# A decoder trunk: last pass of an output projection and its LayerNorms moved into the recurrent stage, with three PSUM banks for its last pieces

## Chip, cores and metric

The kernel runs on one core of a Trainium2 chip. The metric is device time in microseconds. Positions in the trace ("at 1926") are microseconds from the start of the profiled execution's span.

## What is computed

A trunk of two layers over 1024 tokens of width 1024, in float32. Layer 0 mixes tokens by attention, layer 1 by an RWKV-7 recurrence with 12 heads beside 4 memory heads. Each layer merges its heads by an output projection, and each sublayer ends in a LayerNorm:

```python
o = jnp.concatenate([y, o_mem], axis=-1)      # 768 + 256 columns
mix = o @ w_out[1]                            # (1024, 1024)
x = layer_norm(ALPHA * x + mix, ln1_g[1], ln1_b[1])
ff = jnp.square(jax.nn.relu(x @ w_ff1[1])) @ w_ff2[1]
x = layer_norm(ALPHA * x + ff, ln2_g[1], ln2_b[1])
```

Every float32 operand of a matmul is split into a high and a low part, and a product is three matmuls (high by high, high by low, low by high).

## The kernel before

A planner orders the instructions of each engine at build time by program order and its own estimate of when they are ready; each engine's queue is then run in order. `issue_after(m)` queues what it encloses behind `m` on that engine. SyncE (SP) issues the DMAs.

**The recurrent stage** (`rwkv`, L656 to L1246) runs 12 units n = 0 to 11 (two head pairs by 256 tokens). Unit n is prepared two steps ahead (`prepare`, `early`, `late`, `bonus`), its blocks are merged one step ahead (`merge`, PSUM pool `psi`, two banks), then `sequence(n)` runs the recurrence and `finish(n)` (L1188) writes normalised outputs to `o_d` in DRAM. All eight PSUM banks are taken: `psm` 1, `psg` 2, `psi` 2, `psq` 2, `psx` 1.

**Pieces.** Independent work for TensorE is drawn from the generator `project()`: 40 input projections, 16 memory-attention steps and the 48 pieces of `first_out` (L730). `fill(n)` draws n pieces; the table `FILL` (L34) says how many in each unit: 12 before the stage, `FILL[12]` = 7 before the loop, then `FILL[n]` = 4, 4, 3, 4, 4, 4, 11, 11, 12, 12, 11, 6, and `fill(99)` for the rest. All use the one bank of `psm`.

**The output projection.** `first_out` makes three passes over the residual rows `R` (two tiles of 128 x 4 x 1024), with two of the eight 128-row blocks of `w_out` each: blocks 0, 1, then 2, 3, then 6, 7 ("third group"). For each of eight row tiles tt and two column halves nh, `out_part` (L1248) makes one piece: six matmuls of 512 columns (`mm3`, L149 to L151), then one add into `R` (L1255 or L1257). Blocks 4, 5 belong to the last units; their weights are loaded and split after all pieces (L1243), and the rows of `o_d` fetched (`fetch_o`, L345 to L349: a DMA into a `raw` buffer, then `split`: a cast on ScalarE, L143, and a subtraction on VectorE, L144). `raw` buffers: two (`wr`); split pairs for weights: two (`wp`).

**The last pass** runs in the next stage, `out_and_ff` (L1276), layer 1: `out_row` (L1260) does both halves into a double bank of the pool `pso` (two of them) with one add of 1024 columns (L1271). After each second row tile `norm` (L1383) runs `normalise2` on a pair of row tiles: four statistics (L217), two aggregates (L218), 14 small operations (L220 to L228) on VectorE, two scalings on ScalarE (L230), and a store to `n_d`. For the first four row tiles `first_half` adds transposes (`columns`, L241, with copies on ScalarE, L244) and splits. `ahead` loads and splits the first weights of the feed-forward into the memory of `R`'s first half, and `second_half` transposes the rest, with early products pinned between.

The lines that decide the order before:

```python
                fill(99)
                self.wo = [self.load_split(...) for k in (4, 5)]
                for kt in (4, 5):
                    self.fetch_o(kt, kt - 2, slice(0, QT * 3))
```

Of the kernel before, what the change touches and what calls it, by code (L numbers as in the profile page):

```python
# [10 lines left out]
F32 = mybir.dt.float32  # L11
# [9 lines left out]
P = 128  # L21
T = 1024
# [44 lines left out]
class Trunk:  # L67
# [588 lines left out]
    def rwkv(self, rows_src):  # L656
# [8 lines left out]
        with ExitStack() as so:  # L665
# [43 lines left out]
            def project():  # L709
# [15 lines left out]
                yield from remember()  # L725
                yield from first_out()


            def first_out():
                R = self.R = Halves(self.x_tile("h", 1, F32), self.x_tile("l", 1, F32))  # L730
                self.Xh, self.Xl = Halves(self.x_tile("h", 0)), Halves(self.x_tile("l", 0))
                for ks, src in (((0, 1), 0), ((2, 3), 2), ((0, 1), 6)):
                    for k in ks:
                        self.fetch_o(src + k % 2, k)
                    wo = [self.load_split(a["w_out"][1, (src + k % 2) * P : (src + k % 2 + 1) * P, :], (1024,)) for k in ks]
                    for tt in range(KT):
                        if src == 0:
                            nc.sync.dma_start(R[:, tt, :], res_src[tt * P : (tt + 1) * P, :])
                        for nh in range(2):
                            self.out_part(psm, R, tt, nh, ks, wo, src == 0)  # L740
                            yield 1


# [56 lines left out]
            def fill(n):  # L800
                for _ in range(n):
                    if next(pieces, 0) == 0:
                        break
# [99 lines left out]
                psms[:] = [psm]  # L903
            with ExitStack() as s:
                kp = pool(s, "k")
                lp = pool(s, "ld", 2)
                tp = pool(s, "t")
                up = pool(s, "u", 2)
                psg = pool(s, "psg", 2, space=PSUM)
                psi = pool(s, "psi", 2, space=PSUM)  # L910
                psq = pool(s, "psq", 1, space=PSUM)
# [13 lines left out]

                cmp_ = kp.tile([P, P], F32, name="cmpk")
                self.pad(kp, 96)
                self.pad(tp, 96)
                ARK = [kp.tile([P, 2, NC, 2, P], F32, name=f"ARK{i}") for i in range(2)]
                nc.gpsimd.memset(cmp_, 0.0)  # L930
# [256 lines left out]
                def finish(n):  # L1187
                    d = DU.pop(n)  # L1188
                    pa, gs = d["pa"], d["gs"]
                    y8 = d["yd"].rearrange("p u c i -> p (u c) i")  # L1190
                    gt = tp.tile([P, 2, QT], F32, name="gt")
                    nc.sync.dma_start(gt, lo_d[pa : pa + 2].rearrange("u (j i) t -> i u j t", i=P)[:, :, 2, gs])
                    mn = sm.tile([P, 8], F32, name="mn")
                    vr = sm.tile([P, 8], F32, name="vr")
                    nc.vector.tensor_reduce(mn, y8, axis=AX.X, op=ALU.add)
                    nc.vector.tensor_scalar(mn, mn, 1.0 / CH, None, op0=ALU.mult)
                    nc.vector.tensor_sub(y8, y8, mn[:, :, None].broadcast_to([P, 8, CH]))
                    ysq = tp.tile([P, 8, CH], F32, name="ysq", tag="o")
                    nc.scalar.activation(ysq, y8, AF.Square)
                    nc.vector.tensor_reduce(vr, ysq, axis=AX.X, op=ALU.add)  # L1200
                    nc.vector.tensor_scalar(vr, vr, 1.0 / CH, 64e-5, op0=ALU.mult, op1=ALU.add)
                    rs2 = self.rsqrt(vr, 8, "gn")
                    nc.vector.tensor_mul(y8, y8, rs2[:, :, None].broadcast_to([P, 8, CH]))
                    o = tp.tile([P, 2, QT], F32, name="o", tag="o")
                    po = psg.tile([P, 2, NC, CH], F32, name="ps_yo", tag="g")
                    for u in range(2):
                        for c in range(NC):
                            for R, hd in HD:
                                nc.tensor.matmul(po[R, u, c, :], d["yd"][R, u, c, :], self.ident[R, R], start=True, stop=True)
                    for u in range(2):  # L1210
                        j = pa + u
                        nc.scalar.activation(c3(o[:, u, :]), po[:, u], AF.Identity, scale=self.col("gng", j), bias=self.col("gnb", j))
                    nc.vector.tensor_add(o, o, d["bv"])
                    nc.vector.tensor_mul(o, o, gt)
                    nc.sync.dma_start(self.o_d[pa * P : (pa + 2) * P, gs].rearrange("(u i) t -> i u t", i=P), o)
# [12 lines left out]
                for n in range(N):  # L1228
                    sequence(n)
                    if n + 1 < N:  # L1230
                        merge(n + 1, steps[1])
                    if n + 2 < N:
                        prepare(n + 2)
                        early(n + 2)
                        late(n + 2)
                    finish(n)
                    if n + 2 < N:
                        bonus(n + 2)
                    for c, m in enumerate(anchors):
                        with self.tc.issue_after(m):  # L1240
                            fill((FILL[n] + c) // NC)
                fill(99)
                self.wo = [self.load_split(a["w_out"][1, k * P : (k + 1) * P, :], (1024,)) for k in (4, 5)]  # L1243
                for kt in (4, 5):
                    self.fetch_o(kt, kt - 2, slice(0, QT * 3))


    def out_part(self, psm, R, tt, nh, ks, wo, first):  # L1248
        nc = self.nc
        ts_, ns = slice(tt * P, (tt + 1) * P), slice(nh * H, (nh + 1) * H)  # L1250
        ps = psm.tile([P, H], F32, name="ps_o", tag="mm")
        for k, (wh, wl) in zip(ks, wo):
            self.mm3(ps, self.Xh[:, k, ts_], self.Xl[:, k, ts_], wh[:, ns], wl[:, ns], k == ks[0], k == ks[-1])
        if first:
            nc.vector.scalar_tensor_tensor(R[:, tt, ns], R[:, tt, ns], ALPHA, ps, op0=ALU.mult, op1=ALU.add)  # L1255
        else:
            nc.vector.tensor_add(R[:, tt, ns], R[:, tt, ns], ps)  # L1257
# [17 lines left out]

    def out_and_ff(self, layer, res_src, res_dst, last, R=None):  # L1276
        nc, a = self.nc, self.a
        n_d = self.dp.tile([T, D], F32, name=f"n_d{layer}")
# [8 lines left out]
        with ExitStack() as s:  # L1287
# [10 lines left out]
            with ExitStack() as s1:  # L1298
# [70 lines left out]
                with ExitStack() as s2:  # L1369
# [11 lines left out]


                    def norm(tt):  # L1383
                        chain.append(self.normalise2(rows_of(tt)))
                        nc.sync.dma_start(n_d[tt * P : (tt + 2) * P, :].rearrange("(t p) d -> p t d", p=P), rows_of(tt))

                    def first_half(tt):
                        cs, es, i = span(tt)
                        norm(tt)
# [27 lines left out]
                    if R is None:  # L1417
# [9 lines left out]
                        for h in (0, 4):  # L1427
                            for tt in range(h, h + 4):
                                self.out_row(pso, R, tt, range(4), wo, True)
                            for tt in range(h, h + 4):  # L1430
                                self.out_row(pso, R, tt, range(4, 8), wo[4:], False)
                                if tt % 2:
                                    (first_half if tt < 4 else norm)(tt - 1)
                            if h == 0:
                                ahead(0)
                                ahead(1)
                    else:
                        K1 = new(0), new(1)
                        region = lambda i: self.x_tile("hl"[i], 1)

                        self.fetch_o(4, 2, slice(QT * 3, T))
                        self.fetch_o(5, 3, slice(QT * 3, T))
                        for tt in range(KT):
                            self.out_row(pso, R, tt, (2, 3), self.wo, False)
                            if tt % 2:
                                (first_half if tt < 4 else norm)(tt - 1)
                            if tt == 3:
                                ahead(0)
                                ahead(1)
                    s4.close()  # L1450
                    psB = pool_of(s1)("psB", 4, space=PSUM)
                    cut = lambda t, c: (t[0][:, :, c], t[1][:, :, c])
# [477 lines left out]
```

## Time and profile before

| | |
|---|---|
| median of 3 runs | 2670.86 us (2668.06 to 2672.97) |
| profiled execution | 2670.26 us, span 2667.5 us |
| busy share of the span | TensorE 94%, weight loads 76%, VectorE 68%, ScalarE 45%, GpSimd 8% |
| recurrent stage, until its last piece | about 1380 to 1966 us |
| last pass and first LayerNorms | 1966 to 2021 us |

An engine's busy time counts its instructions; matmuls overlap, so a busy TensorE is not one at its peak. In a timeline row stand the start, the time of the (merged) instructions, the engine, the line, the operation, output and inputs, shapes and count, and in brackets the idle time of the engine before it with what ended it.

### The profile page before, as it was taken

What the parts mean: (1) busy time and instruction counts of PE and PEld (TensorE: products, weight loads), DVE (VectorE), ACT (ScalarE), POOL (GpSimd) and SP (SyncE); (2) the same over time, 40 slices, a digit from 0 to 9 for tenths busy, and PEclk for the clock granted to TensorE, in tenths of its full rate; (3) what the DMA queues carried; (4) which work ended last, traced back from release to release, by engine and by line L of the source; (5) the groups of instructions that cost most, each with busy time, mean ns of one, the idle gap of its engine ahead of it and who ended that gap; (6) DMA issues with size and microseconds to landing.
All of it is one profiled execution on the core that took longest, in us unless ns stands there. A gap on an engine that the chain in (4) does not pass through costs nothing. (4 is left out here: it accounts for less than half of the span.)

```text
span 2667.5 us, 41854 instructions
## 1 busy us (share of the span) xinstructions
PE 2519.3 (94%) x16189; PEld 2034.7 (76%) x16189; DVE 1804.9 (68%) x3275; ACT 1192.0 (45%) x1960; POOL 214.9 (8%) x525
## 2 busy tenths in 40 slices
PE   8999999999999999999998999889867999999998
PEld 7877776778888788887876778777555888878886
DVE  5567766577656687676346777897657666568677
ACT  4465555254444433357443343563107444443343
POOL 0012232000000000000012121212000000000000
PEclk9999999999999999999998999999997999999999
DMA  4100001334443777545552333343114544396761
GB/s 170 58 26 17 9 21 59 127 111 159 151 152 142 276 264 267 186 146 185 196 142 78 111 92 106 99 122 103 60 32 142 178 149 151 131 339 233 262 237 64
DMA packets 274966, 370.53 MB, mean 139 GB/s; under 512 B 53776, under 2 KB 152464, under 8 KB 274768
## 3 DMA queue, kind: packets, MB, share of 16 engines
q1 hardware_dynamic: 274624, 367.61, 40.3%
q8 instruction: 127, 2.08, 0.3%
q14 instruction: 71, 0.58, 0.1%
q10 hardware_dynamic: 144, 0.26, 0.0%
HBM read 258.75 MB, written 109.05 MB: 138 GB/s over the span
## 5 line engine op out<-in xcount | busy, mean ns | idle before, releaser
L143 ACT CAST Xh<-wraw 128x1024 fp32r<-128x1024 f32 (+1 forms) x138 | 140.0, 1038 | 216.0 <-PE ps_z L1650 72.7
L149 PE MATMUL ps_in<-Xh,whi 128*128 128x512 f32 x480 | 195.3, 409 | 13.5 <-ACT whi L143 8.2
L150 PE MATMUL ps_in<-Xl,whi 128*128 128x512 f32 x480 | 193.0, 402 | 0.5 <-DVE Xl L144 0.5
L151 PE MATMUL ps_in<-Xh,wlo 128*128 128x512 f32 x480 | 193.2, 403 | 0.0
L143 ACT CAST Xl<-wraw 128x1024 fp32r<-128x1024 f32 x103 | 105.0, 1050 | 156.2 <-PE ps_z L1650 61.8
L144 DVE TENSOR_TENSOR Xh<-wraw,Xh 128x1024 fp32r<-128x1024 f32 x115 | 137.7, 1218 | 50.2 <-ACT Xh L143 49.8
L143 ACT CAST whi<-wraw 128x1024 fp32r<-128x1024 f32 (+3 forms) x95 | 90.3, 954 | 179.7 <-PE ps_o L151 61.1
L144 DVE TENSOR_TENSOR wlo<-wraw,whi 128x1024 fp32r<-128x1024 f32 (+3 forms) x95 | 107.9, 1137 | 68.4 <-ACT whi L143 67.8
L144 DVE TENSOR_TENSOR Xl<-wraw,Xl 128x1024 fp32r<-128x1024 f32 x103 | 123.4, 1219 | 41.2 <-ACT Xl L143 40.8
L149 PEld LDWEIGHTS ps_in<-Xh,whi 128*128 128x128 f32 x480 | 92.4, 192 | 35.1 <-ACT whi L143 8.2
L1315 PE MATMUL ps_f<-Xh,N 128*128 128x512 f32 x320 | 106.7, 397 | 4.9 <-ACT N L143 2.3
L151 PEld LDWEIGHTS ps_in<-Xh,wlo 128*128 128x128 f32 x480 | 92.4, 193 | 20.1 <-issue 0.7
L150 PEld LDWEIGHTS ps_in<-Xl,whi 128*128 128x128 f32 x480 | 92.6, 193 | 19.6 <-DVE Xl L144 1.0
L625 ACT ACTIVATE E<-ps_s,mx,SC 128x128 f32<-128x128 f32 (+7 forms) x96 | 79.4, 831 | 51.1 <-DVE mx L623 24.3
L628 POOL TENSOR_TENSOR E<-E,l 128x768 f32<-128x768 f32 (+5 forms) x60 | 83.8, 1400 | 201.7 <-DVE l L626 101.3
L149 PE MATMUL ps_o<-whi,Xh 128*128 128x512 f32 x160 | 69.5, 434 | 26.7 <-DVE Xh L1257 10.3
L1315 PE MATMUL ps_f<-TB,N 128*128 128x512 f32 x384 | 91.9, 389 | 0.4 <-ACT N L143 0.4
L1650 PE MATMUL ps_y<-Xh 128*128 128x512 f32 x384 | 90.1, 389 | 0.0
L1650 PE MATMUL ps_z<-Xh 128*128 128x512 f32 x384 | 89.6, 389 | 0.0
L1650 PE MATMUL ps_z<-Xl 128*128 128x512 f32 x384 | 89.6, 389 | 0.0
L1650 PE MATMUL ps_y<-Xh,Xh 128*128 128x512 f32 x360 | 85.0, 390 | 0.0
L1315 PEld LDWEIGHTS ps_f<-TB,N 128*128 128x128 f32 x384 | 72.0, 188 | 15.7 <-ACT N L143 0.8
(520 smaller groups left out, 6544.5 us busy)
## 6 DMA issues: line engine op xcount, KB each, us to landing
wraw<-in_w_ff_dram SPq DMA_DIRECT2D x182, 512.0 KB
wraw<-h_d SPq DMA_DIRECT2D x108, 512.0 KB
h_d<-slot SPq DMA_DIRECT2D x128, 256.0 KB
h_d<-tr SPq DMA_DIRECT2D x64, 256.0 KB
wraw<-in_w_in_dram SPq DMA_DIRECT2D x31, 512.0 KB
lo_d<-l_st SPq DMA_DIRECT2D x36, 256.0 KB
rkv_d<-rkv_st SPq DMA_DIRECT2D x36, 256.0 KB
wraw<-in_w_out_dram SPq DMA_DIRECT2D x16, 512.0 KB
```

The lines of the kernel that those rows point to most:

```text
L143: h = self.nc.scalar.copy(hi, src)
L144: l = self.nc.vector.tensor_sub(lo, src, f32(hi))
L149: mm(ps, wh, xh, start=first, stop=False)
L150: mm(ps, wh, xl, start=False, stop=False)
L151: mm(ps, wl, xh, start=False, stop=last)
L625: nc.scalar.activation(E3[:, g, :], S[:, g * w0 : g * w0 + n], AF.Exp, bias=mx[:, g : g + 1], scale=SC[:, i : i + 1], accum_out=l[:, g : g ...
L628: nc.gpsimd.tensor_mul(E3, E3, l[:, :, None].broadcast_to([P, nh, n]))
L1315: yield nc.tensor.matmul(ps, A[x][:, k, :], B[y][:, k, :], start=fresh and k == 0 and i == 0, stop=k == 3 and i == 2, skip_group_check=True)
L1650: m = nc.tensor.matmul(ps[t], A[x][:, u, t * P : (t + 1) * P], B[y][:, u, :], start=fresh and i == u == j == 0, stop=end and i == last_ an ...
```

## The change

The last pass and all its LayerNorms move to the end of the recurrent stage. There they are made by `out_part`, one bank and one 512-column add per piece. A rotation `bank()` chooses the bank: `psm` alone until unit 11, from then on `psm` and the two banks of `psi`, in turn. The weights of blocks 4, 5 get split buffers of their own, `wz`, where the pools `lp` and `tp` were; these close after the last unit is prepared, and three tiles of `finish` (`gt`, `ysq`, `o`) move from `tp` to `up`, which is opened before them. The loads, and the fetch of the first 768 columns, now stand at the end of unit 10; the last 256 columns are fetched at row tile 6. In `out_and_ff` layer 1 keeps the two `first_half` calls and the two `ahead` calls. Layer 0 keeps its order of work.

```diff
@@ rwkv
+            banks = [(psm, "mm")]
+            def bank():
+                banks.append(banks.pop(0))
+                return banks[-1][0].tile([P, H], F32, name="ps_o", tag=banks[-1][1])
@@ first_out
-                            self.out_part(psm, R, tt, nh, ks, wo, src == 0)
+                            self.out_part(bank(), R, tt, nh, ks, wo, src == 0)
@@ the units' pools
-                lp = pool(s, "ld", 2)
-                tp = pool(s, "t")
                 up = pool(s, "u", 2)
+                sx = s.enter_context(ExitStack())
+                lp = pool(sx, "ld", 2)
+                tp = pool(sx, "t")
...
+                self.pad(up, 64)
@@ finish (ysq and o likewise)
-                    gt = tp.tile([P, 2, QT], F32, name="gt")
+                    gt = up.tile([P, 2, QT], F32, name="gt", bufs=1)
@@ the loop over units
                     if n + 2 < N:
                         bonus(n + 2)
+                    if n + 2 == N - 1:
+                        sx.close()
+                        wz = pool(s, "wz", 2)
+                    if n == N - 1:
+                        banks += [(psi, "i"), (psi, "i")]
                     for c, m in enumerate(anchors):
                         with self.tc.issue_after(m):
                             fill((FILL[n] + c) // NC)
+                    if n == N - 2:
+                        wo = [self.load_split(a["w_out"][1, k * P : (k + 1) * P, :], (1024,), wz) for k in (4, 5)]
+                        for kt in (4, 5):
+                            self.fetch_o(kt, kt - 2, slice(0, QT * 3))
                 fill(99)
-                self.wo = [self.load_split(a["w_out"][1, k * P : (k + 1) * P, :], (1024,)) for k in (4, 5)]
-                for kt in (4, 5):
-                    self.fetch_o(kt, kt - 2, slice(0, QT * 3))
+                R = self.R
+                self.n_d = self.dp.tile([T, D], F32, name="n_d1")
+                for tt in range(KT):
+                    if tt == 6:
+                        for kt in (4, 5):
+                            self.fetch_o(kt, kt - 2, slice(QT * 3, T))
+                    for nh in range(2):
+                        self.out_part(bank(), R, tt, nh, (2, 3), wo, False)
+                    if tt % 2:
+                        self.chain = self.norm(R, tt - 1, self.n_d)
@@ out_and_ff, layer 1
-                        self.fetch_o(4, 2, slice(QT * 3, T))
-                        self.fetch_o(5, 3, slice(QT * 3, T))
-                        for tt in range(KT):
-                            self.out_row(pso, R, tt, (2, 3), self.wo, False)
-                            if tt % 2:
-                                (first_half if tt < 4 else norm)(tt - 1)
-                            if tt == 3:
-                                ahead(0)
-                                ahead(1)
+                        chain.append(self.chain)
+                        for tt in (0, 2):
+                            first_half(tt)
+                        ahead(0)
+                        ahead(1)
```

`norm` becomes a method with the same body; `first_half` no longer calls it.

## Rows read from the trace of the kernel before

**Rows 1.** Windows by stage: length; busy us per engine with counts; granted clock; DMA.

```profile
1926.00:1966.00 40.00, 27.54 (x127) 17.48 (x127) 13.97 (x21) 2.45 (x4) 0.00 (x0) 1.00 0.10 33
1966.00:1971.00 5.00, 0.00 (x0) 0.00 (x0) 2.22 (x2) 1.34 (x2) 0.00 (x0) 0.78 0.48 146
1971.00:1996.00 25.00, 24.20 (x96) 19.43 (x96) 21.28 (x44) 1.70 (x4) 0.00 (x0) 0.91 0.19 56
1996.00:2021.00 25.00, 12.06 (x44) 8.26 (x45) 13.29 (x54) 22.31 (x31) 0.00 (x0) 0.57 0.41 168
2021.00:2071.00 50.00, 39.42 (x167) 30.70 (x166) 44.56 (x51) 29.61 (x42) 0.00 (x0) 0.91 0.38 116
```

**Rows 2.** Timeline, third group: its first and last adds, and its last piece's first matmul.

```profile
1928.70 0.69 DVE L1257 TENSOR_TENSOR Xh<-Xh,ps_o 128x512 f32<-128x512 f32 x1 [1.06 <-PE ps_o L151]
...
1963.57 0.50 PE L149 MATMUL ps_o<-whi,Xh 128*128 128x512 f32 x1 [0.78 <-DVE Xl L1257]
...
1965.27 0.69 DVE L1257 TENSOR_TENSOR Xl<-Xl,ps_o 128x512 f32<-128x512 f32 x1 [1.75 <-PE ps_o L151]
```

**Rows 3.** Timeline from the third group to the last pass, several engines.

```profile
1964.57 1.99 ACT L143 CAST whi<-wraw 128x1024 fp32r<-128x1024 f32 x2 [35.50 <-PE ps_o L151]
...
1965.87 2.35 DVE L144 TENSOR_TENSOR wlo<-wraw,whi 128x1024 fp32r<-128x1024 f32 x2
1967.12 7.09 SPq L348 DMA_DIRECT2D wraw<-o_d  x4
1970.22 0.83 ACT L143 CAST Xh<-wraw 128x768 fp32r<-128x768 f32 x1 [3.66 <-DMA wraw<-o_d]
...
1971.11 0.80 PE L149 MATMUL ps_o<-whi,Xh 128*128 128x512 f32 x1 [5.88 <-ACT Xh L143]
...
1972.13 0.63 PE L149 MATMUL ps_o<-whi,Xh 128*128 128x512 f32 x1
...
1972.55 0.63 PE L150 MATMUL ps_o<-wlo,Xh 128*128 128x512 f32 x1
```

**Rows 4.** Timeline of TensorE in the last pass: a matmul and the sixth after it.

```profile
1986.98 0.39 PE L149 MATMUL ps_o<-whi,Xh 128*128 128x512 f32 x1
...
1988.34 0.39 PE L149 MATMUL ps_o<-whi,Xh 128*128 128x512 f32 x1
```

**Rows 5.** Timeline of VectorE: adds of the last pass and the LayerNorms.

```profile
1977.42 1.22 DVE L1271 TENSOR_TENSOR Xh<-Xh,ps_o 128x1024 f32<-128x1024 f32 x1 [0.43 <-PE ps_o L151]
...
1978.67 1.29 DVE L217 BATCH_NORM_STATS2 ln_st<-Xh 128x6 f32<-128x512 f32 x2
...
1984.76 0.15 DVE L220 TENSOR_SCALAR ln_t<-ln_mv 128x2 f32<-128x2 f32 x1
...
1995.34 1.22 DVE L1271 TENSOR_TENSOR Xl<-Xl,ps_o 128x1024 f32<-128x1024 f32 x1
...
1998.47 0.15 DVE L228 SCALAR_TENSOR_TENSOR ln_t<-ln_mv,ln_y 128x2 f32<-128x2 f32 x1
...
2001.06 0.17 DVE L220 TENSOR_SCALAR ln_t<-ln_mv 128x2 f32<-128x2 f32 x1 [1.39 <-ACT Xh L230]
...
2004.01 0.15 DVE L228 SCALAR_TENSOR_TENSOR ln_t<-ln_mv,ln_y 128x2 f32<-128x2 f32 x1
...
2005.89 0.16 DVE L228 SCALAR_TENSOR_TENSOR ln_t<-ln_mv,ln_y 128x2 f32<-128x2 f32 x1
```

**Rows 6.** Timeline of ScalarE: the first scalings, and the second half's first copies.

```profile
1998.65 4.63 ACT L230 ACTIVATE Xh<-Xh,ln_t,ln_y 128x1024 f32<-128x1024 f32 x4 [22.13 <-DVE ln_t L228]
...
2020.76 1.94 ACT L244 ACTIVATE x<-ps_tr,vec 128x256 f32<-128x256 f32 x4
```

**Rows 7.** Timeline: third group's weights cast, and SP's loads of blocks 4, 5.

```profile
1923.31 1.99 ACT L143 CAST whi<-wraw 128x1024 fp32r<-128x1024 f32 x2 [3.39 <-PE ps_o L151]
...
1925.93 2.08 SPq L113 DMA_DIRECT2D wraw<-in_w_out_dram  x2
```

**Rows 8.** DMA view, 1924 to 1944 us: rate in 40 slices of half a microsecond.

```profile
GB/s 0 0 0 0 0 8 98 287 418 262 131 164 369 328 66 18 344 166 12 0 0 0 0 0 0 0 0 0 0 0 0 0 0 0 0 0 0 0 0 0
```

More of the change, by code (lines that the diff above doesn't have):

```diff
@@ L1197, in finish @@
                     nc.vector.tensor_sub(y8, y8, mn[:, :, None].broadcast_to([P, 8, CH]))
-                    ysq = tp.tile([P, 8, CH], F32, name="ysq", tag="o")
+                    ysq = up.tile([P, 8, CH], F32, name="ysq", tag="o", bufs=1)
                     nc.scalar.activation(ysq, y8, AF.Square)
@@ L1203, in finish @@
                     nc.vector.tensor_mul(y8, y8, rs2[:, :, None].broadcast_to([P, 8, CH]))
-                    o = tp.tile([P, 2, QT], F32, name="o", tag="o")
+                    o = up.tile([P, 2, QT], F32, name="o", tag="o", bufs=1)
                     po = psg.tile([P, 2, NC, CH], F32, name="ps_yo", tag="g")
@@ L1241, in rwkv, with norm, out_part @@
                             fill((FILL[n] + c) // NC)
-                fill(99)
-                self.wo = [self.load_split(a["w_out"][1, k * P : (k + 1) * P, :], (1024,)) for k in (4, 5)]
-                for kt in (4, 5):
-                    self.fetch_o(kt, kt - 2, slice(0, QT * 3))
-    def out_part(self, psm, R, tt, nh, ks, wo, first):
+                    if n == N - 2:
+                        assert sum(FILL) - FILL[N - 1] + 12 >= 40 + 16 + 32
+                        wo = [self.load_split(a["w_out"][1, k * P : (k + 1) * P, :], (1024,), wz) for k in (4, 5)]
+                        for kt in (4, 5):
+                            self.fetch_o(kt, kt - 2, slice(0, QT * 3))
+                fill(99)
+                R = self.R
[8 more added lines that the diff above has]
+                        self.chain = self.norm(R, tt - 1, self.n_d)
+    def norm(self, R, tt, n_d):
+        r = R.t[tt // 4][:, tt % 4 : tt % 4 + 2, :]
+        chain = self.normalise2(r)
+        self.nc.sync.dma_start(n_d[tt * P : (tt + 2) * P, :].rearrange("(t p) d -> p t d", p=P), r)
+        return chain
+    def out_part(self, ps, R, tt, nh, ks, wo, first):
         nc = self.nc
         ts_, ns = slice(tt * P, (tt + 1) * P), slice(nh * H, (nh + 1) * H)
-        ps = psm.tile([P, H], F32, name="ps_o", tag="mm")
         for k, (wh, wl) in zip(ks, wo):
@@ L1277, in out_and_ff @@
         nc, a = self.nc, self.a
-        n_d = self.dp.tile([T, D], F32, name=f"n_d{layer}")
+        n_d = self.dp.tile([T, D], F32, name=f"n_d{layer}") if R is None else self.n_d
         h_d = self.dp.tile([7 * NFF // 2 * P, H], F32, name=f"h_d{layer}")
@@ L1383, in norm @@
                     def norm(tt):
-                        chain.append(self.normalise2(rows_of(tt)))
-                        nc.sync.dma_start(n_d[tt * P : (tt + 2) * P, :].rearrange("(t p) d -> p t d", p=P), rows_of(tt))
+                        chain.append(self.norm(R, tt, n_d))
                     def first_half(tt):
                         cs, es, i = span(tt)
-                        norm(tt)
                         for q, K in enumerate((K0, K1)):
@@ L1432, in out_and_ff @@
                                 if tt % 2:
-                                    (first_half if tt < 4 else norm)(tt - 1)
+                                    norm(tt - 1)
+                                    if tt < 4:
+                                        first_half(tt - 1)
                             if h == 0:
@@ L1439, in out_and_ff @@
                         region = lambda i: self.x_tile("hl"[i], 1)
-                        self.fetch_o(4, 2, slice(QT * 3, T))
-                        self.fetch_o(5, 3, slice(QT * 3, T))
-                        for tt in range(KT):
-                            self.out_row(pso, R, tt, (2, 3), self.wo, False)
-                            if tt % 2:
-                                (first_half if tt < 4 else norm)(tt - 1)
-                            if tt == 3:
-                                ahead(0)
-                                ahead(1)
+                        chain.append(self.chain)
[3 more added lines that the diff above has]
+                        ahead(1)
                     s4.close()
```

## The prediction, made before the change was built

> **What bounds the kernel now.** The windows by stage come first [rows 1]. TensorE fills the long stages before and after, but from 1926 to 2021 us it does not: it is busy 27.5 of 40 us, then 0 of 5, then 24.2 of 25, then 12.1 of 25. VectorE is busy 14.0, 2.2, 21.3 and 13.3 us in the same four stretches, ScalarE 2.5, 1.3, 1.7 and 22.3. So four limits follow one another, and each needs its own reading.
>
> The timeline of 1926 to 1966 shows the first [rows 2]. A piece is six matmuls into the only bank of `psm`, and one VectorE add that empties it. The first add of the third group starts at 1928.70, the sixteenth at 1965.27: (1965.27 - 1928.70)/15 = 2.44 us a piece. TensorE waits 0.78 us for the add, the add waits 1.75 us for the matmuls: with one bank the two take turns. In the next stage the same six matmuls have two double banks and come every 1988.34 - 1986.98 = 1.36 us [rows 4]. The turn-taking costs 1.08 us a piece.
>
> The second limit is the bubble [rows 3]: the weights of k = 4, 5 could not be split before the third group's last matmul, since both pairs of split buffers were taken (ScalarE waited 35.5 us); their raw buffers were held, so the fetch of the attention rows started at 1967.12, was cast at 1970.22, and TensorE resumed at 1971.11 after 5.88 us. It ran there at a granted 1.2 GHz: matmuls 0.42 us apart (1972.13 to 1972.55), not 0.23.
>
> The third is VectorE's in-order queue [rows 5]. The first add of the last pass starts at 1977.42, but the first LayerNorm's small operations, from 1984.76, end only at 1998.47: 13.7 us for a chain that takes 2004.01 - 2001.06 = 2.95 us when nothing stands between, because a large add or a pair of statistics (1.29 us) sits between most steps. The fourth is ScalarE [rows 6]: it waits 22.13 us for that first scale and bias, and is then full from 1998.65 until 2020.76, when the second half of the transposes begins: 22.1 us without a gap. What comes behind keeps VectorE busy 44.6 of 50 us [rows 1].
>
> **The change, part by part.** The sum is made against the profiled run (2670.26 us, span 2667.5); the median, 2670.86, lies 0.6 above.
>
> *Banks.* How many pieces get three banks is counted in the code: 12 + 7 + 80 = 99 of the 104 pieces are drawn before the extra banks are added; 40 projections, 16 memory steps and two groups of 16 make 88, so 11 pieces of the third group stay on `psm`. The remaining 5 and the 16 of the last pass turn round three banks, seven of them on `psm`. Two orders are possible for TensorE's queue, which the planner writes. If later pieces fill the gaps, `psm` takes 11 + 7 = 18 turns of 2.44 us: the last add starts at 1928.70 + 17 x 2.44 = 1970.2, and 32 x 1.36 = 43.5 us of matmuls fit beside it. If the order of the program holds, it is 1928.70 + 10 x 2.44 + 21 x 1.36 = 1981.7. Today the last add starts at 1995.34 [rows 5]. I take the first order, since the same rows show the planner putting later work between the steps of an earlier chain; with two microseconds allowed for operands the matmuls end about 1973.
>
> The Trainium skill, TensorE: Matmul & The Clock Gate, section HAM oscillation, reports a kernel where double-buffered PSUM gave no further gain. By that, all pieces would keep their pitch, and the sum would be rival 2's upper end; the measured 2.44 against 1.36 us speaks against it here.
>
> *Weights and operands.* The new buffers lie in memory of the unit pools, which close once the last unit is prepared, so the wait on split buffers goes. What is late next are the raw buffers: two, held by the third group's weights until their casts at 1923.31 [rows 7]. The loads of k = 4, 5 leave at 1925.93 as today; by the transfer rates of the half microseconds that follow, all traffic has landed by 1933.5, this pair near 1931.5 [rows 8]. Two casts (1.99 us) and two subtractions (2.35 us for both) overlap and end near 1934; from the fetch to the first matmul today's way takes 1971.11 - 1967.12 = 4.0 us, and the second tile comes a microsecond behind [rows 3]: operands from about 1939. The last pass needs them at 1939 at the earliest, and in program order after 1955. So these four loads, two late fetches, their casts and subtractions cost nothing on the path: ScalarE is busy 2.5 of those 40 us, VectorE 14.0. Without that cover it would be the bubble of today, 5.9 us, and the slow clock behind it. On SP they stand near the store of the last unit and four stores of normalised rows; those follow ScalarE and nobody in this stage waits for them. The loads of the next weights behind them are wanted some 20 us later.
>
> *Smaller adds.* Sixteen adds of 512 columns (0.69 us) replace eight of 1024 (1.22): 16 x 0.69 - 8 x 1.22 = 1.3 us more VectorE work, beside TensorE. New tiles for `gt`, `o` and `ysq` have the old counts: nothing.
>
> *LayerNorms.* The first pair of rows needs four pieces of the last pass. With gaps filled, the one of them on `psm` is the fourteenth turn of that bank: its add starts at 1928.70 + 13 x 2.44 = 1960.4 and ends near 1961.1; the last statistic (half of 1.29 us) and its aggregate bring it to 1962. The small chain then takes between 2.95 us (undisturbed) and 13.7 us (as today). I take 13.7: adds and statistics of the other rows will be ready in just this stretch, as they were. First scale and bias at 1975.7, against 1998.47: 22.8 us earlier. The bounds: 1965 with the short chain (33.5 us); in program order the fourth piece's add starts at 1928.70 + 10 x 2.44 + 9 x 1.36 = 1965.3, so 1967 + 13.7 = 1980.6 (17.9 us).
>
> *ScalarE.* Its 22.1 us are the same eight scalings, sixteen column copies and six casts. Started at 1976 they end at 1998 instead of 2020.76, if nothing else is late: all norms must be out of VectorE, and from the first add to the last scale they took 2005.89 - 1977.42 = 28.5 us, so 1986 to 1990 from a first add between 1957 and 1961; the column buffers may lie where the new weights lie, and then wait for the last matmul, 1973 or 1982, before ScalarE turns to them at 1978 or 1983. Neither is late. What follows is the code of before and moves as a whole.
>
> Sum: 22.8 earlier, less half a microsecond for the added VectorE work = 22.3. 2670.86 - 22.3 = **2648.5 us**.
>
> **Rivals.**
> 1. *Program order on TensorE.* The planner finishes the third group first: gain 18, 2653. For it: eleven pieces still take turns on one bank, and priority follows the program. Chance 0.22.
> 2. *VectorE becomes the bound.* A pair of rows costs it 4 adds, 4 statistics and the small chain, 4 x 0.69 + 4 x 0.64 + 2.95 = 8.3 us, or 2.1 us a piece, hardly under today's 2.44: banks come free late. At 2.44 throughout, the fourth piece of the last pass has its add at 1928.70 + 19 x 2.44 = 1975.1 and the chain ends at 1976.6 + 13.7 = 1990.3, gain 8, 2662; at 2.1 after the eleventh piece it is 1928.70 + 10 x 2.44 + 9 x 2.1 = 1972, so 1987, gain 11, 2659. For it: 21.3 busy of 25 us today. Chance 0.15.
> 3. *The first norm runs undisturbed*, since matmuls deliver adds only every 1.36 us: gain up to 33 by its own chain, 29 if the last norm holds ScalarE; 2640. Chance 0.14.
> 4. *Slower: the clock falls.* If TensorE were granted 1.2 GHz from 1927 on while banks alternate, the 32 pieces would take 32 x 6 x 0.42 = 80.6 us and end at 2007.6, 12.3 us behind today's last add at 1995.34; VectorE, with time to spare, would trail it by some 5 us (the last statistics and one chain) instead of today's 2005.89 - 1995.34 = 10.6, so the loss is about 6.7: 2677. It decides from (2001 - 1927)/32 = 2.3 us a piece, 0.385 us a matmul. Against it: a single bank with 69% busy kept 1.00 from 1926 to 1966; the clock fell only after the empty 5 us, and again around 2000, where TensorE waited for ScalarE [rows 1, 3]. Chance 0.05. The Trainium skill, TensorE: Matmul & The Clock Gate, section on a second failure mode, says that cycling through PSUM banks with small idle spells can make the clock swing; no row here shows it.
> 5. *It does nothing measurable.* The stage behind gives the time back, because its weights or VectorE's 44.6 of 50 us are not ready sooner, or banks and loads are planned so that the last pass starts where it did: 2668. Against it: between 1996 and 2021 VectorE is free 11.7 us, and the loads wait for row buffers that come free earlier. Chance 0.06.
>
> **How the numbers follow.** The forecast has 0.38. 0.2% is 5.3 us, about what a measurement of this kernel tells from no change. Faster: 0.38 + 0.22 + 0.15 + 0.14 = 0.89; same 0.06; slower 0.05. The range takes in rivals 1 and 2 with a little for operands, and most of 3: 2638 to 2662.
>
> **What would show it.** Right: L1257's adds of the last pieces closer than 2.44 us; no wait of 5.88 us before the last pass; the fetch of the attention rows near 1932; the first scaling on ScalarE near 1976 and the second half of the transposes near 1998; every later stage shifted by that. Wrong: a last pass after 1982, a first scaling after 1990, a granted clock of 0.5 between 1940 and 1975, or an idle stretch between the norms and the first early products longer than today's.

## The result, and the profile after

| | median of 4 runs | ratio to before | profiled span |
|---|---|---|---|
| before, measured beside it | 2670.84 us (2668.06 to 2672.97) | | 2667.5 us |
| changed kernel | 2650.31 us (2646.72 to 2652.60) | 0.9923 (0.9905 to 0.9940) | 2647.8 us |

The change saves 20.5 us, 0.77%. Predicted were 2648.5 us, in a range of 2638 to 2662.

In the changed kernel the adds of `out_part` have line L1290 (L1257 before). The first four windows of [rows 1], now of the changed kernel:

```profile
1926.00:1966.00 40.00, 36.58 (x181) 28.83 (x182) 27.34 (x41) 5.50 (x8) 0.00 (x0) 1.00 0.28 86
1966.00:1971.00 5.00, 4.22 (x20) 3.17 (x19) 3.09 (x5) 0.00 (x0) 0.00 (x0) 1.00 0.00 0
1971.00:1996.00 25.00, 12.27 (x52) 7.99 (x50) 18.09 (x79) 14.07 (x19) 0.00 (x0) 0.80 0.31 126
1996.00:2021.00 25.00, 19.30 (x84) 14.66 (x84) 16.18 (x18) 20.36 (x33) 0.00 (x0) 0.79 0.39 130
```

TensorE is busy 36.58 of the first 40 us instead of 27.54, at a granted 1.00, and 4.22 of the next 5 instead of 0: turn-taking and bubble are mostly gone. From 1971 to 1996 it falls to 12.27 of 25, since the last pass is nearly through. ScalarE begins its full stretch in that window (14.07 us busy instead of 1.70).

The stage behind the recurrence shifts by several us from one profiled execution to the next. Positions below are therefore also given from a zero Z that lies ahead of the work that the edits move (except in the two kernels with four banks): the start of the second group's last add, at 1924.01 before and 1924.51 after. Its row before:

```profile
1924.01 0.69 DVE L1257 TENSOR_TENSOR Xl<-Xl,ps_o 128x512 f32<-128x512 f32 x1 [0.28 <-PE ps_o L151]
```

The timeline of VectorE, changed kernel. First the add at Z; then the third group's first and third add of the bank `psm`; one on the way; the last of the first pair's four pieces; the first and last small operation of that pair's norm; and the last add:

```profile
1924.51 0.69 DVE L1290 TENSOR_TENSOR Xl<-Xl,ps_o 128x512 f32<-128x512 f32 x1 [0.26 <-PE ps_o L151]
...
1930.33 0.69 DVE L1290 TENSOR_TENSOR Xh<-Xh,ps_o 128x512 f32<-128x512 f32 x1 [2.19 <-PE ps_o L151]
...
1938.37 0.69 DVE L1290 TENSOR_TENSOR Xh<-Xh,ps_o 128x512 f32<-128x512 f32 x1 [0.57 <-PE ps_o L151]
...
1956.58 1.41 DVE L1290 TENSOR_TENSOR Xl<-Xl,ps_o 128x512 f32<-128x512 f32 x2 [2.03 <-PE ps_o L151]
...
1969.89 0.69 DVE L1290 TENSOR_TENSOR Xh<-Xh,ps_o 128x512 f32<-128x512 f32 x1 [0.67 <-PE ps_o L151]
...
1971.59 0.17 DVE L220 TENSOR_SCALAR ln_t<-ln_mv 128x2 f32<-128x2 f32 x1
...
1981.04 0.16 DVE L228 SCALAR_TENSOR_TENSOR ln_t<-ln_mv,ln_y 128x2 f32<-128x2 f32 x1
...
1982.23 0.68 DVE L1290 TENSOR_TENSOR Xl<-Xl,ps_o 128x512 f32<-128x512 f32 x1
```

The first add stands at Z + 5.8 (before, [rows 2], at Z + 4.7). The fourth piece of the last pass has its add at 1969.89, the very last add is at 1982.23. The chain takes 1981.04 - 1971.59 = 9.5 us, where [rows 5] had 13.7.

The timeline of TensorE, changed kernel: the first matmul of each of the last four pieces.

```profile
1970.63 0.50 PE L149 MATMUL ps_o<-whi,Xh 128*128 128x512 f32 x1 [0.78 <-DVE Xh L1290]
...
1973.07 0.50 PE L149 MATMUL ps_o<-whi,Xh 128*128 128x512 f32 x1 [0.78 <-DVE Xh L1290]
...
1976.37 0.50 PE L149 MATMUL ps_o<-whi,Xh 128*128 128x512 f32 x1 [1.65 <-DVE Xh L1290]
...
1980.05 0.50 PE L149 MATMUL ps_o<-whi,Xh 128*128 128x512 f32 x1 [2.02 <-DVE Xl L1290]
```

From 1957.32 to 1969.46 matmuls follow one another without a gap. Then each of these pieces first waits for the add of the piece before: they are the last pass's pieces on `psm`, alone at the end, taking turns as in [rows 2]. Two of the waits are longer than there (1.65 and 2.02 us instead of 0.78), because VectorE is busy with the norms as well: 9.69 of the 10 us from 1971 to 1981.

The timeline of SP and ScalarE, changed kernel: the fetch of attention rows, its first cast, the first scaling, and the first copy of the second half of the transposes.

```profile
1932.23 3.26 SPq L348 DMA_DIRECT2D wraw<-o_d  x2
...
1935.31 0.83 ACT L143 CAST Xh<-wraw 128x768 fp32r<-128x768 f32 x1 [1.60 <-DMA wraw<-o_d]
...
1981.23 2.37 ACT L230 ACTIVATE Xh<-Xh,ln_t,ln_y 128x1024 f32<-128x1024 f32 x2 [38.57 <-DVE ln_t L228]
...
2003.02 1.08 ACT L244 ACTIVATE x<-ps_tr,vec 128x256 f32<-128x256 f32 x2
```

The fetch leaves at 1932.23 instead of 1967.12 [rows 3]. The first scaling comes at 1981.23, Z + 56.7, against 1998.65, Z + 74.6 [rows 6]; the second half at 2003.02, Z + 78.5, against 2020.76, Z + 96.75. In absolute positions the second half is 17.7 us earlier, and the span 19.7 shorter; the other 2.0 us come later.

### The profile page after: what moved, and what is told of

The parts are those of the page before. It is cut to its first block, busy times and chain, and to the rows that moved or that the text cites. A ratio compares the mean times of both kernels' runs of the same rounds, so it can differ in the third digit from the quotient of the medians.

```text
span 2647.8 us, 41865 instructions
## 1 busy us (share of the span) xinstructions
PE 2511.0 (95%) x16189; PEld 2032.6 (77%) x16189; DVE 1806.0 (68%) x3283; ACT 1192.7 (45%) x1960; POOL 215.5 (8%) x525
## 5 line engine op out<-in xcount | busy, mean ns | idle before, releaser
L1348 PEld LDWEIGHTS ps_f<-TB,N 128*128 128x128 f32 x384 | 72.0, 188 | 15.6 <-ACT N L143 0.7
L1678 PEld LDWEIGHTS ps_z<-Xl 128*128 128x128 f32 x384 | 72.1, 188 | 14.9
```

Source lines behind the costliest of these rows:

```text
L1348: yield nc.tensor.matmul(ps, A[x][:, k, :], B[y][:, k, :], start=fresh and k == 0 and i == 0, stop=k == 3 and i == 2, skip_group_check=True)
L1678: m = nc.tensor.matmul(ps[t], A[x][:, u, t * P : (t + 1) * P], B[y][:, u, :], start=fresh and i == u == j == 0, stop=end and i == last_ an ...
```

## The experiments

Each kernel ran beside the kernel before, whose medians were 2673.18 us (experiments 1 to 4), 2674.58 (5 to 8) and 2671.03 (9).

### 1. The move without the banks

```diff
-                    if n == N - 1:
-                        banks += [(psi, "i"), (psi, "i")]
```

> The changed kernel with the two extra banks taken out of the rotation: all pieces, the last pass too, use the one bank of psm. Theory A (turn-taking on a bank sets when the first LayerNorm can start, and ScalarE's 22 us follow it): pieces stay 2.44 us apart, the fourth piece of the last pass is added near 1975, its norm's small chain takes 9.5 to 13.7 us, first scaling 1986 to 1990 instead of 1981 in the changed kernel; 2655 to 2662 us. Theory B (the gain came from the early operands and from moving the norms; more banks give nothing): 2650 us as the changed kernel.

Measured: 2669.86 us, ratio 0.9989 (0.9978 to 1.0001): nothing, less than either theory expected. Its timeline (VectorE and ScalarE): Z, the first three pairs' scalings, the first column copies, the last add, the second half.

```profile
1917.21 0.69 DVE L1288 TENSOR_TENSOR Xl<-Xl,ps_o 128x512 f32<-128x512 f32 x1 [0.27 <-PE ps_o L151]
...
1976.47 2.38 ACT L230 ACTIVATE Xh<-Xh,ln_t,ln_y 128x1024 f32<-128x1024 f32 x2 [41.56 <-DVE ln_t L228]
...
1986.21 2.37 ACT L230 ACTIVATE Xh<-Xh,ln_t,ln_y 128x1024 f32<-128x1024 f32 x2 [7.35 <-DVE ln_t L228]
...
1995.94 2.38 ACT L230 ACTIVATE Xl<-Xl,ln_t,ln_y 128x1024 f32<-128x1024 f32 x2 [7.36 <-DVE ln_t L228]
...
1998.53 2.85 ACT L244 ACTIVATE tr<-ps_tr,vec 128x256 f32<-128x256 f32 x6 [0.21 <-PE ps_o L150]
...
1998.70 0.69 DVE L1288 TENSOR_TENSOR Xl<-Xl,ps_o 128x512 f32<-128x512 f32 x1 [1.02 <-PE ps_o L151]
...
2012.75 1.08 ACT L244 ACTIVATE x<-ps_tr,vec 128x256 f32<-128x256 f32 x2
```

Pieces keep 2.43 us each to the end, so the last add stands at Z + 81.5 (before, [rows 5], at Z + 71.3). The first scaling is early, Z + 59.3, but the next ones come 9.7 us apart, waiting for their pairs' norms (7.35 us of idle ScalarE each), and the first column copies start at 1998.53, released by the last pass's matmuls. The second half starts at Z + 95.5, only 1.2 us earlier than before. A rule I had used, "first scaling + 22 us", holds only while neither the last pair nor the last matmul comes later. The early operands are worth nothing when 16 more pieces must take turns on one bank.

### 2. The banks without the move

The kernel before, with three banks for the whole third group, and the last pass where it was:

```diff
+                    if n == N - 2:
+                        banks += [(psi, "i"), (psi, "i")]
-                            self.out_part(psm, R, tt, nh, ks, wo, src == 0)
+                            self.out_part(bank(), R, tt, nh, ks, wo, src == 0)
```

> The kernel before with one part of the change alone: the third group's 16 pieces turn round three banks; the last pass, its operands and norms stay in the next stage. Theory A: the third group ends near 1928 + 16 x 1.36 = 1950 instead of 1966; the bubble of 5.9 us and all behind it move up as they are; about 2655 us. Theory B: the last pass waits for its operands anyway, 2670 us.

Measured: 2654.38 us, ratio 0.9928 (0.9912 to 0.9945), as the first theory had it. Its timeline: Z, the third group's last add, the last pass's first add, the first scaling, the second half.

```profile
1925.56 0.69 DVE L1264 TENSOR_TENSOR Xl<-Xl,ps_o 128x512 f32<-128x512 f32 x1 [0.28 <-PE ps_o L151]
...
1950.74 0.69 DVE L1264 TENSOR_TENSOR Xl<-Xl,ps_o 128x512 f32<-128x512 f32 x1 [0.67 <-PE ps_o L151]
...
1962.46 1.22 DVE L1278 TENSOR_TENSOR Xh<-Xh,ps_o 128x1024 f32<-128x1024 f32 x1
...
1983.70 4.64 ACT L230 ACTIVATE Xh<-Xh,ln_t,ln_y 128x1024 f32<-128x1024 f32 x4 [21.77 <-DVE ln_t L228]
...
2005.81 1.95 ACT L244 ACTIVATE x<-ps_tr,vec 128x256 f32<-128x256 f32 x4
```

The third group ends at Z + 25.2 instead of Z + 41.3, and the whole stage behind it moves up by that: second half at Z + 80.25, 16.5 us earlier. The bubble stays: 1962.46 - 1950.74 = 11.7 us from add to add. So banks alone give as much as the whole change measured. The two are not the same banks, though: here all 16 pieces of the third group have three, in the changed kernel only the last 5. With the banks placed as here, the move on top is worth 0.9874/0.9928 = 0.9946, some 14 us (experiment 4).

### 3. Banks and move, operands late

The changed kernel without `wz`: weights and rows of blocks 4, 5 are loaded, split and fetched behind `fill(99)`, in the old buffers.

```diff
-                    if n == N - 2:
-                        wo = [self.load_split(..., (1024,), wz) for k in (4, 5)]
-                        for kt in (4, 5):
-                            self.fetch_o(kt, kt - 2, slice(0, QT * 3))
                 fill(99)
+                wo = [self.load_split(..., (1024,)) for k in (4, 5)]
+                for kt in (4, 5):
+                    self.fetch_o(kt, kt - 2, slice(0, QT * 3))
```

> The changed kernel without split buffers of its own for the last weights: they are loaded, split and the rows fetched after all pieces of the third group, in the old buffers; banks and place of the last pass as changed. Theory A: third group ends near 1958, the bubble of 6 to 7 us returns, but then the last pass runs in order at 1.36 us with no backlog on psm: fourth piece near 1970, first scaling near 1981; 2649 to 2652 us, about the changed kernel's. Theory B: the early operands carried the gain, so 2656 us or more.

Measured: 2662.53 us, ratio 0.9961 (0.9948 to 0.9973), as the second theory had it. Its timeline: Z, the third group's last add, the first matmul of the last pass, its add.

```profile
1928.98 0.69 DVE L1286 TENSOR_TENSOR Xl<-Xl,ps_o 128x512 f32<-128x512 f32 x1 [0.26 <-PE ps_o L151]
...
1964.86 0.69 DVE L1286 TENSOR_TENSOR Xl<-Xl,ps_o 128x512 f32<-128x512 f32 x1 [1.75 <-PE ps_o L151]
...
1970.75 0.80 PE L149 MATMUL ps_o<-whi,Xh 128*128 128x512 f32 x1 [5.92 <-ACT Xh L143]
...
1977.58 1.88 DVE L1286 TENSOR_TENSOR Xh<-Xh,ps_o 128x512 f32<-128x512 f32 x3 [0.86 <-PE ps_o L151]
```

The bubble is back (5.92 us on TensorE), and from its first matmul to the first add it takes another 6.8 us (1970.75 to 1977.58), so 12.7 from add to add. I had counted the first part alone. Against the changed kernel the early operands are worth 10 us by the ratios (0.9961 against 0.9923, with intervals apart) and 12 by the medians (2662.53 - 2650.31, each from its own series).

### 4. Three banks for the whole third group as well

```diff
-                    if n == N - 1:
+                    if n == N - 2:
                         banks += [(psi, "i"), (psi, "i")]
```

> The changed kernel with the two extra banks added one unit earlier (end of unit 10), so that all 16 pieces of the third group and the 16 of the last pass turn round three banks. Theory A: psm has no backlog of 13 pieces in front of the last pass; 32 pieces at 1.36 us end near 1973 instead of 1982, the first norm's four pieces are in by 1960, first scaling 1969 to 1973, second half of the transposes 1991 to 1995; 2639 to 2643 us. Theory C (VectorE or ScalarE sets the first scaling, whatever the banks): 2650 us.

Measured: 2640.26 us, ratio 0.9874 (0.9856 to 0.9891), as the first theory had it. Its timeline: Z, the first small operation of the first pair's norm, the last add of all, that norm's last operation, the second half.

```profile
1920.72 0.69 DVE L1290 TENSOR_TENSOR Xl<-Xl,ps_o 128x512 f32<-128x512 f32 x1 [0.26 <-PE ps_o L151]
...
1954.03 0.15 DVE L220 TENSOR_SCALAR ln_t<-ln_mv 128x2 f32<-128x2 f32 x1
...
1967.66 0.69 DVE L1290 TENSOR_TENSOR Xl<-Xl,ps_o 128x512 f32<-128x512 f32 x1
...
1969.60 0.14 DVE L228 SCALAR_TENSOR_TENSOR ln_t<-ln_mv,ln_y 128x2 f32<-128x2 f32 x1
...
1991.90 2.86 ACT L244 ACTIVATE x<-ps_tr,vec 128x256 f32<-128x256 f32 x6
```

No piece waits behind a backlog any more: the last add is at Z + 46.9 instead of Z + 57.7, the second half at Z + 71.2. But the first pair's chain now takes 1969.60 - 1954.03 = 15.6 us, with adds, statistics and small operations of the other rows between its steps.

### 5. The place of the norms in the program

```diff
-                    if tt % 2:
-                        self.chain = self.norm(R, tt - 1, self.n_d)
@@ out_and_ff, layer 1
-                        chain.append(self.chain)
                         for tt in (0, 2):
+                            norm(tt)
                             first_half(tt)
+                        norm(4)
+                        norm(6)
```

> The changed kernel, with the norms and the half transposes issued where the kernel before has them (after the recurrent stage) and everything else as in the changed kernel. Theory A (the place of the norms in the program decides little, since the order is written by when things can run): the first scaling within 2 us of the changed kernel's 56.7 us behind the last add of the second group, time 2647 to 2654 us. Theory B (the norms in the recurrent stage carry a part of the gain): the norms slip behind other work of VectorE and ScalarE, the first scaling comes 4 us later or more, and the time is 2655 us or more.

Measured: 2650.12 us, ratio 0.9905 (0.9882 to 0.9929). The planner writes the same order, instruction for instruction, on TensorE, VectorE and ScalarE as for the changed kernel; the first scaling is at Z + 56.6. So moving the norms in the program does nothing by itself; when they can run decides. This run also serves as the changed kernel's time beside experiments 6 to 8.

### 6. No piece of the last pass behind the backlog

```diff
                 fill(99)
+                banks[:] = [(psi, "i"), (psi, "i")]
```

> The changed kernel with no piece of the last pass on the bank psm: the last pass turns between the two new banks alone. Theory A (the last pass's pieces on psm stand behind the 13 pieces of the third group there, and the fourth of them held the first norm back to 1969.9 us): the first pair's four pieces are in some 33 to 40 us behind the second group's last add instead of 45.4, the first scaling comes 46 to 52 us behind it instead of 56.7, and the time is 2640 to 2647 us. Theory B (TensorE's total work decides, in whatever order the pieces come, or the first norm only waits longer for VectorE): the first scaling stays within 3 us of 56.7 and the time is 2648 to 2653 us.

Measured: 2637.27 us, ratio 0.9861 (0.9834 to 0.9888), below the range of the first theory, and 0.9861/0.9905 = 0.9956, 11.8 us, under the changed kernel as run beside it (experiment 5). Its timeline: Z, the first scaling, the first column copies, the second half.

```profile
1929.43 0.69 DVE L1291 TENSOR_TENSOR Xl<-Xl,ps_o 128x512 f32<-128x512 f32 x1 [0.26 <-PE ps_o L151]
...
1962.51 2.38 ACT L230 ACTIVATE Xh<-Xh,ln_t,ln_y 128x1024 f32<-128x1024 f32 x2 [14.62 <-DVE ln_t L228]
...
1980.13 2.85 ACT L244 ACTIVATE tr<-ps_tr,vec 128x256 f32<-128x256 f32 x6 [6.18 <-PE ps_o L150]
...
1996.60 1.07 ACT L244 ACTIVATE x<-ps_tr,vec 128x256 f32<-128x256 f32 x2
```

The first scaling comes at Z + 33.1 instead of Z + 56.7, earlier than I had worked out (46 to 52). The column copies then wait 6.18 us for a matmul of `ps_o`, as in the first experiment, and start at Z + 50.7; the second half at Z + 67.2, 11.3 us earlier than in the changed kernel, which is the time gained. This run tests what the failed step of the prediction cost (below).

### 7. Each pair's norm behind the pair before

The kernel of experiment 4, with

```diff
                     if tt % 2:
-                        self.chain = self.norm(R, tt - 1, self.n_d)
+                        with self.tc.issue_after(self.chain) if tt > 1 else ExitStack():
+                            self.chain = self.norm(R, tt - 1, self.n_d)
```

> Three banks for the whole third group, and each pair's norm put behind the chain of the pair before on VectorE, so that the first chain does not share the engine with the statistics of the later pairs. Theory A (the first norm's 15.6 us chain is stretched by the later pairs' statistics and adds in VectorE's order, and its end sets the half transposes): the chain takes 5 to 10 us, the first scaling comes 43 to 46 us behind the second group's last add instead of 49.1, and the time is 2634 to 2640 us against 2640.3. Theory B (what stretches the chain are the adds and splits, which stay, or the last norm then binds): the second half of the transposes starts within 2 us of 71.2 us and the time is 2639 to 2643 us.

Measured: 2635.73 us, ratio 0.9851 (0.9825 to 0.9878). Its timeline: Z, the first chain's first and last small operation, the first scaling, the second half.

```profile
1930.35 0.69 DVE L1291 TENSOR_TENSOR Xl<-Xl,ps_o 128x512 f32<-128x512 f32 x1 [0.26 <-PE ps_o L151]
...
1963.16 0.17 DVE L220 TENSOR_SCALAR ln_t<-ln_mv 128x2 f32<-128x2 f32 x1
...
1969.72 0.15 DVE L228 SCALAR_TENSOR_TENSOR ln_t<-ln_mv,ln_y 128x2 f32<-128x2 f32 x1
...
1969.91 2.38 ACT L230 ACTIVATE Xh<-Xh,ln_t,ln_y 128x1024 f32<-128x1024 f32 x2 [20.15 <-DVE ln_t L228]
...
1994.46 1.08 ACT L244 ACTIVATE x<-ps_tr,vec 128x256 f32<-128x256 f32 x2
```

The chain takes 6.6 us instead of 15.6, the first scaling is at Z + 39.6 (earlier than the 43 to 46 of the first theory) and the second half at Z + 64.1, 7.1 earlier than in experiment 4. Adds still stand between the steps of this chain; the later pairs' statistics and small operations, which the edit takes out of it, were what stretched it. In time the intervals of the two kernels overlap, so that gain is seen in the trace and not settled by the times.

### 8. Four banks, two units earlier

```diff
-                    if n == N - 1:
+                    if n == N - 3:
+                        banks.append((psx, "x"))
+                    if n == N - 2:
                         banks += [(psi, "i"), (psi, "i")]
```

> The changed kernel with the further banks given two units earlier, one bank from the second last unit but one on and two more from the second last unit on, so that the end of the second group alternates too and the third group and the last pass have four banks. Theory A (what counts is how early the pieces ahead of the last pass are through TensorE): the third group's pieces come at 1.36 us each or closer from its first one on, the second half of the transposes starts at least as early as with three banks for the whole third group (71 us behind the second group's last add), and the time is 2632 to 2641 us. Theory B (the extra pieces of TensorE push the last unit's own matmuls and the operands back): the second group's last add comes later and the time is 2642 us or more.

Measured: 2630.50 us, ratio 0.9834 (0.9811 to 0.9856): with experiment 9 the fastest of these kernels, and under the range of the first theory by 1.5 us. One window of it, and then rows of its timeline: the last unit's output, the first matmul that had to wait for it, the last pass's add behind that, the first transposes, the first column copies, the second half.

```profile
1926.00:1946.00 20.00, 20.00 (x99) 16.26 (x95) 16.80 (x41) 1.89 (x3) 0.00 (x0) 1.00 0.00 0
```

```profile
1949.87 1.02 ACT L1220 ACTIVATE o<-ps_yo,vec 128x256 f32<-128x256 f32 x2 [13.83 <-PE ps_yo L1217]
...
1957.87 0.50 PE L149 MATMUL ps_o<-whi,Xh 128*128 128x512 f32 x1 [2.39 <-ACT Xh L143]
...
1962.97 1.28 DVE L1292 TENSOR_TENSOR Xl<-Xl,ps_o 128x512 f32<-128x512 f32 x2 [2.56 <-PE ps_o L151]
...
1963.46 0.60 PE L241 MATMUL ps_tr<-cst,Xh 128*128 128x128 f32 x4
...
1964.15 2.84 ACT L244 ACTIVATE tr<-ps_tr,vec 128x256 f32<-128x256 f32 x6
...
1980.60 1.10 ACT L244 ACTIVATE x<-ps_tr,vec 128x256 f32<-128x256 f32 x2
```

TensorE has no idle time at all in these 20 us. The price: the pieces go ahead of the last unit on TensorE, whose output copy comes at 1949.87 instead of 1930.85 in the changed kernel. Its rows then reach the last pass late: TensorE waits 2.39 us for their cast at 1957.87 and VectorE 2.56 us at 1962.97; TensorE comes to the transposes at 1963.46, behind the last pass's matmuls, and the column copies start at 1964.15. ScalarE's first four scalings end at the same moment, so two limits meet there: the first norms, and the recurrence's last unit.

### 9. Experiments 7 and 8 in one kernel

```diff
+                    if n == N - 3:
+                        banks.append((psx, "x"))
+                    if n == N - 2:
+                        banks += [(psi, "i"), (psi, "i")]
...
+                        with self.tc.issue_after(self.chain) if tt > 1 else ExitStack():
```

> Both together: the banks two units earlier, and each pair's norm behind the chain of the pair before. With the early banks alone the first scaling came at 1959.5 us after a first chain of 16.7 us (1942.7 to 1959.3), and the column copies began at 1964.2, after the last matmul of the last pass, which waits for the last unit's rows. Theory A (the first chain's length still sets the half transposes): the chain takes 5 to 12 us, the four scalings of the first half are done before the last matmul, ScalarE's stretch shortens by some 4 us, and the time is 2624 to 2628 us. Theory B (the last unit's rows, which reach the operands at about 1958 us, are the bound by now, and the pairs behind one another delay the last norm): the second half of the transposes starts within 2 us of 1980.6 and the time is 2629 to 2633 us.

Measured: 2629.64 us (5 runs), ratio 0.9840 (0.9821 to 0.9860), the same as experiment 8 and as the second theory had it in time. Its timeline: the first transposes and the second half.

```profile
1966.81 0.60 PE L241 MATMUL ps_tr<-cst,Xh 128*128 128x128 f32 x4
...
1986.29 1.92 ACT L244 ACTIVATE x<-ps_tr,vec 128x256 f32<-128x256 f32 x4
```

This execution runs 3.5 us behind that of experiment 8 already ahead of the edits (the second group's last add at 1914.74 instead of 1911.22), so 3.5 us have to come off its positions. The first chain did get shorter, from its first aggregate 10.2 us (1946.20 to 1956.35) instead of 16.7, but the transposes start no earlier for it (1966.81 - 3.5 = 1963.3, against 1963.46), the four scalings were not done before them, and nothing was gained: with four banks the last unit's rows hold the transposes. The second half came 5.7 - 3.5 = 2.2 us later than in experiment 8, just outside the 2 us of the second theory.

## Why the prediction was right, and which step was off

The sign, the size (20.5 us measured, 22.3 predicted) and the main mechanism were right. Two errors of opposite sign stand in the sum, and that the total is so close is partly luck: from Z the first scaling came 17.9 us earlier instead of 22.8, and about 2 us that I had not forecast came behind the second half. The first scaling stands about where rival 1 had it (1981.23, against 1980.6), but not by rival 1's way: the fourth piece came later than rival 1 had it (1969.89 instead of 1965.3) and the chain was shorter.

**Banks.** Right: with more than one bank a piece needs TensorE's 1.36 us and not 2.44 [rows 2, 4]; experiments 2 and 4 run at that. The counts of pieces were right too. The Trainium skill, TensorE: Matmul & The Clock Gate, section HAM oscillation, with its kernel that had no further gain from double-buffered PSUM, does not carry over: experiment 2 changes only the banks and saves 0.72%.

**The step that failed** is in "LayerNorms": "the one of them on `psm` is the fourteenth turn of that bank: its add starts at 1928.70 + 13 x 2.44 = 1960.4". It was the fourteenth turn, but at 1969.89. 1.6 us of the 9.5 are a later first add (1930.33). The other 13 x (3.04 - 2.44) = 7.8 are the length of a turn: (1969.89 - 1930.33)/13 = 3.04 us. I had taken the turn of a bank that has TensorE to itself. With the gaps filled it no longer has: a gap of 1.08 us does not hold a piece of 1.36, so each turn that lets a piece of another bank in takes 2 x 1.36 = 2.72, as in (1969.89 - 1956.58)/5 = 2.66. The first two turns took 8.0 us together (1930.33 to 1938.37), beside the operands' arrival. So gaps were filled, as I had it, but the filling was paid by the very bank on which the first norm waited; and once the other banks' pieces had run out, the rest of the last pass took turns alone until 1982.23, by coincidence at the end that I had worked out for program order (1981.7) instead of 1970.2. Experiment 6 shows what the wait behind that bank cost: with the last pass off it the time falls by another 11.8 us.

**The chain**, sized at 13.7 us, took 9.5. Between its steps stand three adds of 0.7 us and nine statistics of other rows, where before there were five adds of 1.22 us and ten statistics: the late pieces came one at a time. VectorE was not idle for that, with 9.69 of 10 us busy from 1971 to 1981. First scaling: predicted 1975.7, measured 1981.23. That its stretched length comes from the other pairs' work is shown by experiment 7 against 4 (6.6 us against 15.6). The 2.95 us that I called undisturbed [rows 5] also hold steps of the next pair's chain.

**Weights and operands.** Right in time: fetch predicted near 1932, seen at 1932.23; operands predicted from 1939, the first matmul on them starts at 1936.20 and the last subtraction of the first 768 columns ends at about 1940. That they cost next to nothing held: TensorE waits 1.6 us for them, once. Their worth I had priced at the bubble's 5.9 us and a slow clock behind it without a figure; it is 10 to 12 us (experiment 3).

**ScalarE.** 22.1 us predicted, 2003.02 - 1981.23 = 21.8 measured. My remark that the column buffers may wait for the last pass's matmuls did not matter here; in experiments 1 and 6 those matmuls release the first column copies.

**Behind the second half.** I had the code move as a whole, less 0.5 us for VectorE's larger share; it gave 2.0 us more. I did not follow these further.

**The rivals.** Program order (1) was half right: it held on one bank, not on the engine. VectorE as the bound (2) is out as long as pieces come from three banks: 27.3 us busy of 40, and its adds mostly wait for TensorE. From 1971 to 1981, where the first chain stands, it is full. An undisturbed norm (3) did not come. The clock (4): granted 1.00 from 1926 to 1971 with three banks in rotation, and 1.00 with four (experiment 8). The Trainium skill, TensorE: Matmul & The Clock Gate, section on a second failure mode, ties a swinging clock to cycling through PSUM banks with small idle spells; these traces don't show it. That nothing would come of it (5) is out for the change, and was true of its move alone (experiment 1).

## What to carry to other kernels

When a serial resource gets company, recount the old queue with the new neighbours: a bank with a backlog turns more slowly once other banks fill the gaps, and a rotation that deals urgent pieces onto it makes them wait for the whole backlog. Give the new banks before the backlog forms, or keep the urgent pieces off the old one. Removing one of two limits in a row can be worth nothing: ask for each part what it gives alone and what it gives on top of the other. Here the move alone gave nothing (ratio 0.9989), the banks for the whole third group alone 0.9928, and the two together 0.9874; given one unit too late, the same banks with the move gave no more than the banks alone.

## What the runs showed of the hardware that I had not expected

TensorE kept a granted 1.00 with no idle time at all for 20 us while four banks turned and VectorE emptied one about every 1.4 us beside statistics and splits (16.80 us busy of the same 20). And the changed kernel and experiments 1 and 3 to 7, whose VectorE and ScalarE do the same work in the same order up to Z, reached Z at between 1917.21 us (experiment 1) and 1930.35 (experiment 7): 13 us between executions that no edit explains, more than half of the change's gain, which is why the differences here were read from Z and the gains from several runs. For the changed kernel and experiment 5, one and the same program in order, it is 1924.51 and 1926.75.
